# Four changes of emission order in a two-block transformer kernel on one core

## The chip, the cores and the metric

One core of one Trainium2 chip runs the whole kernel. Times are device microseconds (us) of one execution. Before the change the median of three runs is 884.3 us (883.33 to 884.74).

## The reference

A sequence of 256 rows of 1024 numbers (f32) goes through two blocks, one after the other. Cut to what the change touches, the first block computes:

```python
h = rmsnorm(x, g_mix_pre);  proj = h @ w_in
y_fox = forgetting_attention(fq, fk, fv, f_logit)         # 8 heads of 64
y_chk = chunked_relpos_attention(cq, ck, cv, rel_bias)    # 8 heads of 64
y = concat(rmsnorm(y_fox, g_fox_out), rmsnorm(y_chk, g_chk_out))
x = x + rmsnorm(y @ w_out, g_mix_post)
h = rmsnorm(x, g_mem_pre)
y = memory_cross_attention(h, rmsnorm(mem, g_mem_kv), w_mq, w_mk, w_mv, w_mo)  # 4 heads of 256
x = x + rmsnorm(y, g_mem_post);  h = rmsnorm(x, g_ff_pre)
y = square(relu(h @ w_ff1)) @ w_ff2
x = x + rmsnorm(y, g_ff_post)
```

The second block is a gated delta rule of 8 heads beside a sparse attention of 8 heads, an output product and a feed-forward part. Of it the change touches the values of the delta rule alone: they are transposed, scaled and stored (tile `vs`) before the first solve reads them.

## The kernel before

**Products.** All big products run on TensorE (PE). Each f32 weight tile (`raw`, 512 KB) comes by a DMA on SP's queue into one of four buffers and is split in two parts: ScalarE (ACT) writes `whi`, VectorE (DVE) then writes `wlo` = raw − whi. Each logical multiply is three matmuls (`mm3`): high by high, high by low, low by high. Activations are split the same way (`xhi`, `xlo`, or `xb`, which holds both). The 256 rows are two halves of 128, A and B. A product with rows as output (`gemm_n_skew`, tags `gs` and `mo`) computes all of half A first and then half B with the same weight parts, which are held in the meantime (`k.held`); `gemm_n_inter` (`gn`) alternates the halves. In both, `mm_n` does two steps of three 128x512 matmuls for one weight part, "a unit" below, with a `k.tick()` after each step.

**Order of the work.** The program is straight-line code, so each engine runs its instructions in the order in which Python emits them. Products are the main line. Everything else (heads, norms, transposes) is a generator, a "side": it runs until a `yield`, which names what it waits for. At each tick `Kern.tick` (L261) steps every side once whose due time has passed by a planner's clock, which advances with each emitted matmul by a fixed cost (three 128x512 matmuls are 0.64 us, three of 256 columns 0.32); the planner also keeps end times of ACT, DVE, POOL and DMA work. A yielded float means "due so many us after the clock now" (L253). Sides of rank −1 (the post chains) are stepped first. `k.finish` (L272) runs the named sides to their end at once, however late.

**Splits.** `Kern.pump` (L313) emits the `whi` and `wlo` of parts to come, each time the main line takes a part or drops a held one (`part`, `drop`). While a side of rank −1 lives it stops at four parts ahead. `refill` issues the DMA of the next raw tile when a split has been emitted. So the splits stand in the queues of ACT and DVE among the instructions of the chains, in the order of emission.

**What the change touches.**

- *Fox and chunked attention heads*, `head_pairs.rest` (L863 to 867): weights, transposes of `p` into a bank `tb`, DVE's copy to `pt`, then `attn_pv` (L671): three matmuls `o` from `pt` and the values. The heads run beside the `gt` products (steps of three 128x256 matmuls).
- *Post chains*, `chain_post` (L498 to 528) with `post_chain` (L976). For one half: squares of the product (`junk`, ACT), `yg` (DVE), a reciprocal root on POOL, `x` (DVE), squares again, `xg` (DVE), a second root `rs`, then `chain_xt` (L467): DVE scales `xg` by `rs` in place, PE transposes it in two groups of four (`tb`), and ACT and DVE split each group into `xb`. Two products use it ahead of a product that reads the result: `w_out` (`gs`, L990), after whose half B the second half of the memory values (`gn`, L991) fills PE before `k.finish(*st.values())` (L992) and the `mq` product (`gt`); and `w_mo` (`mo`), after which the feed-forward's `gs` follows, its half A behind `k.finish(st2[0])` (L1070) and its half B behind `k.finish(st2[1])` (`before_b`, L1073).
- *Memory heads and the `mo` product* (L998 and L1039 to 1059). Head 3 is the last; its `ops` matmuls are emitted as a side, and `k.finish(st[3])` stands before the units with i = 3, which read its output (`xhi`, `xlo` of `ot`). Half A: units (j, i) = (0,0), (0,1), (0,2), (1,0), (1,1), (1,2), then (0,3), (1,3); half B the same.
- *Values of the delta rule*, `chain_v` (L1622): for each of two groups and each half, four transposes of `vc` into `tb` and DVE's scaling into `vs`. `chain_gdn` (L1746) joins these sides before the first `solve`, whose matmuls are `wp`.

Of the kernel before, what the change touches and what calls it, by code (L numbers as in the profile page):

```python
# [23 lines left out]
A, B = 0, 1  # L24
# [14 lines left out]
def hs(half):  # L39
    return slice(half * P, half * P + P)  # L40
# [320 lines left out]
def split(k, hi, lo, src, scale=None):  # L361
    nc = k.nc
    if scale is None:
        nc.scalar.copy(hi, src)
        nc.vector.tensor_tensor(lo, src, hi.bitcast(F32), op=OP.subtract)
    else:
        nc.scalar.activation(hi, src, AF.Copy, scale=scale)
        nc.vector.scalar_tensor_tensor(lo, src, scale, hi.bitcast(F32), op0=OP.mult, op1=OP.subtract)
# [26 lines left out]
def mm_n(k, ps, xt, half, p, kt0, w=512, c0=0):  # L395

    for r in range(2):
        kt = kt0 + r
        for b, (a, e) in zip(ps, ((c0, c0 + w),) if len(ps) == 1 else ((0, w), (w, 2 * w))):
            k.mm3(b[:, :e - a], xt.x(kt, half), p.at(r, a, e), kt == 0, kt == KT - 1)  # L400
        k.tick()
# [48 lines left out]
def mean_sq(k, srcs, n):  # L450

    ss = k.small(2, "ss")
    for j, s in enumerate(srcs):
        k.nc.scalar.activation(k.junk[:, :s.shape[-1]], s, AF.Square, scale=n ** -0.5, accum_out=ss[:, j:j + 1])
    return ss


def transposes(k, srcs, n=P):

    ps = yield from k.get((P, 4, P), "tb")  # L460
    for j, s in enumerate(srcs):
        k.tr(ps[:, j, :n], s, n)
    yield ps
    return ps


def chain_xt(k, xt, half, xg, rs, kb0=0):  # L467

    nc = k.nc
    for j, g in enumerate(xg):  # L470
        if rs is not None:
            nc.vector.tensor_scalar(g, g, rs, None, op0=OP.mult)
    pend = []
    for j, g in enumerate(xg):
        yield g
        ps = yield from transposes(k, [g[:, i * P:i * P + P] for i in range(4)])
        split(k, xt.hi[kb0 + j][:, :, hs(half)], xt.lo[kb0 + j][:, :, hs(half)], ps)
        k.put()
    yield [t[kb0 + j][:, :, hs(half)] for t in (xt.hi, xt.lo) for j in range(len(xg))]
# [15 lines left out]
    yield from chain_xt(k, xt, half, xg, rs)  # L495


def chain_post(k, half, y, gpost, x_old, x_new, gpre, xt):  # L498


    nc = k.nc
    c = lambda t, j: t[:, j * 512:j * 512 + 512]
    yield y
    if gpost is not None:
        ss = mean_sq(k, y, D)
        yg = k.t4([P, D], name="yg")
        for j in range(2):
            nc.vector.tensor_tensor(c(yg, j), y[j], c(gpost, j), op=OP.mult)
        k.put(2)
        yield ss  # L510
        rs = rstd_col(k, ss, D)
        yield rs
    ss = k.small(2, "ss")
    for j in range(2):
        if gpost is not None:
            nc.vector.scalar_tensor_tensor(c(x_new, j), c(yg, j), rs, c(x_old, j), op0=OP.mult, op1=OP.add)
        else:
            nc.vector.tensor_tensor(c(x_new, j), y[j], c(x_old, j), op=OP.add)
        nc.scalar.activation(k.junk[:, :512], c(x_new, j), AF.Square, scale=D ** -0.5, accum_out=ss[:, j:j + 1])
    if gpost is None:  # L520
        k.put(2)
    xg = k.t4([P, D], name="xg")
    for j in range(2):
        nc.vector.tensor_tensor(c(xg, j), c(x_new, j), c(gpre, j), op=OP.mult)
    yield ss
    rs = rstd_col(k, ss, D)
    yield rs
    yield from chain_xt(k, xt, half, [c(xg, 0), c(xg, 1)], rs)


# [140 lines left out]
def attn_pv(k, pt, v0, v1, o0, o1):  # L671
    k.mm(o0, pt[:, 0], v0)
    k.mm(o1, pt[:, 1], v0, True, False)
    k.mm(o1, pt[:, 2], v1, False, True)
# [34 lines left out]
def block1(k, x, mem, w_in, b_fgt, rel, g_fox_out, g_chk_out, w_out, g_mix_pre, g_mix_post,  # L709
# [4 lines left out]
    x0 = [k.t4([P, D], name="x0") for _ in range(2)]  # L714
# [7 lines left out]
    ht = XT(k)  # L722
# [30 lines left out]
    ps = [norm_t(half, j) for half in range(2) for j in range(2)]  # L753
# [74 lines left out]
    fq, ev = qk_evac(0.125)  # L828
# [3 lines left out]
    fk, ev = qk_evac(1.0)  # L832
# [3 lines left out]
    y = [k.t4([P, D], name="y") for _ in range(2)]  # L836
# [25 lines left out]
    def head_pairs(scores, weights, v, o):  # L862
        def rest(h, s):  # L863
            p = yield from weights(h, s)
            pt = yield from attn_transpose(k, p, nc.vector.tensor_copy)
            c = slice(h * 64, h * 64 + 64)
            attn_pv(k, pt, v[:, 0, c], v[:, 1, c], o[0][:, c], o[1][:, c])

        def pair(i):
            s = yield from scores(i)  # L870
            yield from join([k.add(rest(2 * i + j, s[j])) for j in range(2)])
        return lanes(k, pair, 4, 3)
# [48 lines left out]
    cq, ev = qk_evac(0.125)  # L921
    gemm_t(k, ht, 512, ev)
    ck, ev = qk_evac(1.0)
# [47 lines left out]
    gpo, gmp = gain(k, g_mix_post), gain(k, g_mem_pre)  # L971
# [1 line left out]
    k.finish(s_fox)  # L973


    def post_chain(gpost, x_old, x_new, gpre_, xt):  # L976
        banks, st = {}, {}

        def evac(half, j, ps):
            banks[half, j] = ps[0]  # L980
            if j == 1:
                st[half] = k.add(chain_post(k, half, [banks[half, 0], banks[half, 1]], gpost, x_old[half],
                                            x_new[half], gpre_, xt), rank=-1)
            return True
        return evac, st

    x1 = x0
    ht = XT(k)
    ev, st = post_chain(gpo, x0, x1, gmp, ht)
    gemm_n_skew(k, yt, 2, ev, before_4=lambda: k.finish(s_chk))  # L990
    gemm_n_inter(k, mt, lambda half, ps: nc.scalar.copy(mv[half][:, 1], ps[0]))  # L991
    k.finish(*st.values())  # L992
# [3 lines left out]
    ot = XS(k)  # L996
# [33 lines left out]
    st = {}  # L1030
# [9 lines left out]
    x2 = x1  # L1040
    ht = XT(k)
    ev, st2 = post_chain(gmo, x1, x2, gfp, ht)
    parts = {}
    for half in range(2):
        ps = [k.bank(name="mo") for _ in range(2)]
        for js, iis in ((0, (0, 1, 2)), (1, (0, 1, 2)), (0, (3,)), (1, (3,))):
            if iis == (3,):
                k.finish(st[3])
            for i in iis:
                if half == 0:  # L1050
                    while (js, i) not in parts:
                        n = len(parts)
                        parts[n // 4, n % 4] = k.part()
                        k.held += 1
                else:
                    k.drop()
                mm_n(k, ps[js:js + 1], ot, half, parts[js, i], 2 * i)
        ev(half, 0, ps[0:1])
        ev(half, 1, ps[1:2])


    gfo2, gnx = gain(k, g_ff_post), gain(k, next_gain)
# [105 lines left out]
def block2(k, x3, ht, st, out, conv_w, norm_mlp_g):  # L1168
# [453 lines left out]
    def chain_v(b, sides):  # L1622
        yield from join(s_u)
        tp = yield from transposes(k, [kc[b][:, j, 0:P] for j in range(4)])
        nc.scalar.copy(kns[0][:, 4 * b:4 * b + 4], tp)
        k.put()
        yield from join(sides)
        for half in range(2):
            yield vc[b]
            tp = yield from transposes(k, [vc[b][:, j, hs(half)] for j in range(4)])  # L1630
            nc.vector.tensor_tensor(vs[half][:, 4 * b:4 * b + 4], tp, bc(hnk[:, half, 4 * b:4 * b + 4], P),
                                    op=OP.mult)
            k.put()
# [270 lines left out]
```

## Time and profile before

| | |
|---|---|
| median of the runs | 884.3 us |
| the profiled execution, its own time | 884.03 us |
| its span in the trace | 882.1 us |
| PE busy | 870.4 us (99%) |
| DVE busy | 603.5 us (68%) |
| ACT busy | 465.3 us (53%) |
| granted TensorE clock, whole span | 1.00 |

The span is the stretch from the first to the last instruction; 1.9 us of the execution's time lie outside it. The table says which engine has no room; where its few idle microseconds are, and who causes them, the waits and the timelines say. In a timeline a row is a run of like instructions, with the start of the first, and the number in brackets is the engine's idle time ahead of it and what ended that. The end of a matmul is modelled, so stretches are best read from start to start.

### The profile page before, as it was taken

The page shows a single profiled execution, that of the slowest core. Times are in us where ns is not written, and L with a number is a line of the kernel's source. Part 1 is how long each engine was busy: PE and PEld are TensorE (multiplying, and loading weights), DVE is VectorE, ACT ScalarE, POOL GpSimd, SP SyncE. Part 2 cuts the span into 40 slices and gives each one's busy share as a digit, 9 for nine tenths or more (in the row PEclk, how much of TensorE's full clock was granted, in tenths as well). Part 3 has the DMA queues.
Part 4 walks back from the last instruction along what each step waited for, and adds up shares of the span by engine and source line. Part 5 has one row for each costly group of instructions (what it writes and reads, how often), then busy time and mean ns, then how long its engine had stood idle before and what let it go on. Part 6 is the DMA issues. An engine that isn't in the chain of part 4 may idle for free.

```text
span 882.1 us, 13900 instructions
## 1 busy us (share of the span) xinstructions
PE 870.4 (99%) x5320; PEld 754.0 (85%) x5320; DVE 603.5 (68%) x1061; ACT 465.3 (53%) x837; POOL 89.2 (10%) x148
## 2 busy tenths in 40 slices
PE   7999999999999999999999999999999999999998
PEld 6979998799788888888798899988977888888887
DVE  5675664765687667664768999879567786666661
ACT  6574654554476444443648664553765564444440
POOL 3100010200020000000100138600010000000000
PEclk9999999999999999999999999999999999999999
DMA  8982436473387666654553586485235587666521
GB/s 268 294 246 77 144 120 239 119 262 99 94 242 218 207 201 191 191 191 146 172 161 97 143 188 182 97 230 155 71 95 173 165 252 200 191 191 191 192 96 48
DMA packets 162612, 150.82 MB, mean 171 GB/s; under 512 B 20081, under 2 KB 127217, under 8 KB 162546
## 3 DMA queue, kind: packets, MB, share of 16 engines
q1 hardware_dynamic: 161970, 148.88, 56.9%
q10 hardware_dynamic: 576, 1.05, 0.4%
q8 instruction: 42, 0.69, 0.3%
q14 instruction: 24, 0.20, 0.1%
HBM read 148.08 MB, written 1.84 MB: 170 GB/s over the span
## 4 chain that ended last, share of the span: by engine, by line
PE 90%; DVE 4%; ACT 4%; DMA 1%; issue 1%; POOL 0%; ACTq 0%; DVEq 0%; POOLq 0%
PE gt L212 33%; PE acc L212 20%; PE gn L212 12%; PE gs L212 11%; PE tb L225 3%; PE mo L212 3%; DVE wlo L96 2%; PE o L212 1%; ACT whi L96 1%; PE s L212 1%; PE ops L212 1%; PE ms L212 1%; ACT p L96 1%; DMA raw<-in_w_out_dram 1%; PE qp L212 1%
## 5 line engine op out<-in xcount | busy, mean ns | idle before, releaser
L96 DVE TENSOR_TENSOR wlo<-raw,whi 128x1024 fp32r<-128x1024 f32 (+1 forms) x263 | 315.9, 1224 | 107.9 <-ACT whi L96 98.8
L96 ACT CAST whi<-raw 128x1024 fp32r<-128x1024 f32 (+1 forms) x264 | 269.4, 1048 | 61.0 <-DMA raw<-in_w_in_dram 28.8
L212 PE MATMUL gt<-xb,whi 128*128 128x256 f32 (+1 forms) x1152 | 276.1, 322 | 0.0
L212 PE MATMUL gt<-xb,wlo 128*128 128x256 f32 x768 | 215.0, 280 | 0.0
L212 PEld LDWEIGHTS gt<-xb,whi 128*128 128x128 f32 x1152 | 189.9, 188 | 17.2 <-issue 0.3
L212 PEld LDWEIGHTS gt<-xb,wlo 128*128 128x128 f32 x768 | 144.7, 188 | 0.3
L212 PE MATMUL acc<-wlo,uh 128*128 128x512 f32 (+1 forms) x288 | 106.2, 369 | 0.0
L212 PE MATMUL acc<-whi,ul 128*128 128x512 f32 (+1 forms) x288 | 106.2, 369 | 0.0
L212 PE MATMUL acc<-whi,uh 128*128 128x512 f32 (+1 forms) x288 | 106.1, 368 | 0.0
L212 PE MATMUL gn<-whi,xb 128*128 128x512 f32 x256 | 90.2, 408 | 0.0
L212 PE MATMUL gs<-whi,xb 128*128 128x512 f32 (+1 forms) x288 | 86.3, 375 | 0.5 <-ACT xb L96 0.5
L212 PEld LDWEIGHTS acc<-whi,uh 128*128 128x128 f32 x288 | 54.2, 188 | 10.1
L212 PEld LDWEIGHTS acc<-whi,ul 128*128 128x128 f32 x288 | 54.1, 188 | 9.7
L212 PEld LDWEIGHTS acc<-wlo,uh 128*128 128x128 f32 x288 | 54.1, 188 | 9.5
L96 ACT COPY r<-gt 128x256 f32<-128x256 f32 x48 | 17.8, 370 | 84.0 <-PE gt L212 84.0
L212 PEld LDWEIGHTS gs<-whi,xb 128*128 128x128 f32 x288 | 51.9, 188 | 10.8 <-ACT xb L96 1.0
L212 PEld LDWEIGHTS gn<-whi,xb 128*128 128x128 f32 x256 | 48.2, 188 | 10.9 <-issue 1.0
L96 DVE TENSOR_TENSOR r<-gt,r 128x256 f32<-128x256 f32 x48 | 20.3, 423 | 49.7 <-ACT r L96 48.9
L212 PE MATMUL gs<-wlo,xb 128*128 128x512 f32 (+1 forms) x144 | 53.4, 371 | 0.8 <-DVE wlo L96 0.7
L96 POOL TENSOR_SCALAR ms<-ss 128x1 f32<-128x1 f32 x20 | 9.2, 459 | 422.1 <-ACT junk L96 422.0
L212 PE MATMUL gn<-wlo,xb 128*128 128x512 f32 x128 | 50.3, 393 | 0.0
L96 DVE SCALAR_TENSOR_TENSOR cy<-gt,cw,cy 128x255 f32<-128x255 f32 (+2 forms) x72 | 29.1, 474 | 4.7 <-ACT cy L96 4.6
(379 smaller groups left out, 1215.8 us busy)
## 6 DMA issues: line engine op xcount, KB each, us to landing
raw<-in_w_in_dram SPq DMA_DIRECT2D x84, 512.0 KB, 4.7
raw<-in_w_ff_dram SPq DMA_DIRECT2D x64, 512.0 KB, 4.7
raw<-in_w_mlp_up_dram SPq DMA_DIRECT2D x32, 512.0 KB, 5.6
raw<-in_w_mlp_down_dram SPq DMA_DIRECT2D x32, 512.0 KB, 3.4
raw<-in_w_out_dram SPq DMA_DIRECT2D x16, 512.0 KB, 3.8
raw<-in_w_mk_dram SPq DMA_DIRECT2D x8, 512.0 KB, 5.0
raw<-in_w_mv_dram SPq DMA_DIRECT2D x8, 512.0 KB, 4.0
raw<-in_w_mq_dram SPq DMA_DIRECT2D x8, 512.0 KB, 4.9
```

Of the source, the lines that this page charges most:

```text
L96: f(*args, **kw)
L212: self.nc.tensor.matmul(out, lhsT, rhs, start=start, stop=stop)
L225: self.nc.tensor.transpose(out, in_, self.ident[:n, :n])
```

## The change

Four edits. A side that is about to run `attn_pv` first waits 0.7 us of the planner's clock. The post chain of half A of the `w_out` product waits 2.0 us between its second root and `chain_xt`. In the `mo` product the first unit of half B moves ahead of half A's last two units and ahead of `k.finish(st[3])`. And each half of `chain_v` waits 2.5 us before its transposes.

```diff
@@ def chain_post @@
-def chain_post(k, half, y, gpost, x_old, x_new, gpre, xt):
+def chain_post(k, half, y, gpost, x_old, x_new, gpre, xt, later=0.0):
...
     rs = rstd_col(k, ss, D)
     yield rs
+    if later:
+        yield later
     yield from chain_xt(k, xt, half, [c(xg, 0), c(xg, 1)], rs)
@@ head_pairs.rest @@
             pt = yield from attn_transpose(k, p, nc.vector.tensor_copy)
             c = slice(h * 64, h * 64 + 64)
+            yield 0.7
             attn_pv(k, pt, v[:, 0, c], v[:, 1, c], o[0][:, c], o[1][:, c])
@@ post_chain @@
-    def post_chain(gpost, x_old, x_new, gpre_, xt):
+    def post_chain(gpost, x_old, x_new, gpre_, xt, later=0.0):
...
                 st[half] = k.add(chain_post(k, half, [banks[half, 0], banks[half, 1]], gpost, x_old[half],
-                                            x_new[half], gpre_, xt), rank=-1)
+                                            x_new[half], gpre_, xt, later * (half == A)), rank=-1)
...
-    ev, st = post_chain(gpo, x0, x1, gmp, ht)
+    ev, st = post_chain(gpo, x0, x1, gmp, ht, 2.0)
@@ the mo product @@
-    parts = {}
-    for half in range(2):
-        ps = [k.bank(name="mo") for _ in range(2)]
-        for js, iis in ((0, (0, 1, 2)), (1, (0, 1, 2)), (0, (3,)), (1, (3,))):
-            if iis == (3,):
-                k.finish(st[3])
-            for i in iis:
-                if half == 0:
-                    while (js, i) not in parts:
-                        n = len(parts)
-                        parts[n // 4, n % 4] = k.part()
-                        k.held += 1
-                else:
-                    k.drop()
-                mm_n(k, ps[js:js + 1], ot, half, parts[js, i], 2 * i)
-        ev(half, 0, ps[0:1])
-        ev(half, 1, ps[1:2])
+    parts, mo = {}, {}
+    first = [(js, i) for js in range(2) for i in range(3)]
+    last = [(0, 3), (1, 3)]
+
+    seq = [(A,) + x for x in first] + [(B,) + first[0]] + [(A,) + x for x in last]
+    seq += [(B,) + x for x in first[1:] + last]
+    for half, js, i in seq:
+        if (half, js, i) == (A, 0, 3):
+            k.finish(st[3])
+        if (half, js) not in mo:
+            mo[half, js] = k.bank(name="mo")
+        if half == A:
+            while (js, i) not in parts:
+                n = len(parts)
+                parts[n // 4, n % 4] = k.part()
+                k.held += 1
+        else:
+            k.drop()
+        mm_n(k, [mo[half, js]], ot, half, parts[js, i], 2 * i)
+        if (js, i) == (1, 3):
+            for j in range(2):
+                ev(half, j, [mo[half, j]])
@@ chain_v @@
         for half in range(2):
             yield vc[b]
+            yield 2.5
             tp = yield from transposes(k, [vc[b][:, j, hs(half)] for j in range(4)])
```

## Rows read from the trace of the kernel before

**Rows 1.** Page, part 1: busy time, share of the span, instructions per engine.

```profile
span 882.1 us, 13900 instructions
...
PE 870.4 (99%) x5320; PEld 754.0 (85%) x5320; DVE 603.5 (68%) x1061; ACT 465.3 (53%) x837; POOL 89.2 (10%) x148
```

**Rows 2.** Waits of PE: engine, line, awaited; total us, times, longest.

```profile
PE tb L225 <- DVE xg L96: 1.4, 2, 1.0
...
PE mo L212 <- ACT xhi L96: 0.7, 1, 0.7
```

**Rows 3.** Chain of waits: start us, length us, engine, operation (48 matmuls 128x512).

```profile
145.81 11.13 PE gs L212 x48
```

**Rows 4.** Timeline of PE, 64 to 70 us: start, duration, engine, operation, [idle before].

```profile
67.63 0.27 PE L212 MATMUL gt<-xb,wlo 128*128 128x256 f32 x1
68.40 1.55 PE L212 MATMUL o<-fv,pt 128*128 128x64 f32 x12 [0.49 <-DVE pt L96]
```

**Rows 5.** Timeline of DVE, 66 to 69.5 us.

```profile
67.79 1.48 DVE L96 COPY pt<-tb 128x384 f32<-128x384 f32 x3
```

**Rows 6.** Instructions on tile vs: duration min/median/max ns, first and last start us.

```profile
L212 PE MATMUL wp<-vs,TT x32: 270/275/276, 619.1 to 640.0; 128*128 128x128 f32 x32
...
L96 DVE TENSOR_TENSOR vs<-tb,hnk x4: 683/684/685, 571.0 to 591.1; 128x512 f32<-128x512 f32 x4
```

**Rows 7.** Timeline of PE, 163 to 168 us.

```profile
164.19 0.39 PE L212 MATMUL gs<-whi,xlo 128*128 128x512 f32 x1
165.57 0.63 PE L225 MATMUL tb<-ident,xg 128*128 128x128 f32 x4 [0.99 <-DVE xg L96]
```

**Rows 8.** Timeline of DVE, 156 to 186 us.

```profile
163.80 1.23 DVE L96 TENSOR_TENSOR wlo<-raw,whi 128x1024 fp32r<-128x1024 f32 x1 [0.68 <-ACT whi L96]
164.95 0.88 DVE L96 TENSOR_SCALAR xg<-xg,rs 128x512 f32<-128x512 f32 x2
...
177.56 0.88 DVE L96 TENSOR_SCALAR xg<-xg,rs 128x512 f32<-128x512 f32 x2
```

**Rows 9.** Timeline of PE, 177.5 to 182.5 us.

```profile
178.94 0.60 PE L225 MATMUL tb<-ident,xg 128*128 128x128 f32 x4
...
181.90 0.39 PE L212 MATMUL gt<-xb,whi 128*128 128x256 f32 x2
```

**Rows 10.** Timeline of PE, 224.5 to 231 us.

```profile
226.50 0.40 PE L212 MATMUL mo<-whi,xlo 128*128 128x512 f32 x1
226.92 1.99 PE L212 MATMUL ops<-mpt,mv 128*128 128x256 f32 x8
229.59 0.50 PE L212 MATMUL mo<-whi,xhi 128*128 128x512 f32 x1 [0.68 <-ACT xhi L96]
...
230.31 0.50 PE L212 MATMUL mo<-whi,xlo 128*128 128x512 f32 x1
```

**Rows 11.** Timeline of ACT, 226 to 258 us.

```profile
228.95 0.58 ACT L96 CAST xhi<-ops 128x512 fp32r<-128x512 f32 x1 [3.68 <-PE ops L212]
...
243.33 1.05 ACT L96 CAST whi<-raw 128x1024 fp32r<-128x1024 f32 x1
244.28 0.60 ACT L96 ACTIVATE junk<-mo 128x512 bf16<-128x512 f32 x1
...
253.45 1.05 ACT L96 CAST whi<-raw 128x1024 fp32r<-128x1024 f32 x1 [0.85 <-DMA raw<-in_w_ff_dram]
```

**Rows 12.** Timeline of PE, 244 to 258 us.

```profile
244.75 0.39 PE L212 MATMUL gs<-whi,xb 128*128 128x512 f32 x1
...
255.12 0.60 PE L225 MATMUL tb<-ident,xg 128*128 128x128 f32 x4
...
257.04 0.48 PE L212 MATMUL gs<-whi,xb 128*128 128x512 f32 x1
```

**Rows 13.** Timeline of DVE, 226 to 258 us.

```profile
229.57 0.69 DVE L96 TENSOR_TENSOR xlo<-ops,xhi 128x512 fp32r<-128x512 f32 x1 [2.70 <-ACT xhi L96]
...
253.56 0.94 DVE L96 TENSOR_SCALAR xg<-xg,rs 128x512 f32<-128x512 f32 x2
```

## The prediction

> **What bounds the kernel now.** I read the page's busy times first: PE works 870.4 of 882.1 us [rows 1], so all its idle time together is 11.7 us. No edit adds or removes a matmul or a DMA; all four can only move PE's idle time. The waits of PE say whose it is [rows 2]: transposes that waited for a scaled `xg` (two waits, 1.4 us, the longest 1.0) and the `mo` product that waited for `xhi` (0.7). The timelines place them. At 68.40 the value products `o` follow a step that started at 67.63 [rows 4]; at 165.57 transposes follow a matmul that started at 164.19 [rows 7]; around 227 to 230 the last memory head stalls the `mo` product [rows 10]. A 128x512 matmul takes 0.232 us from start to start (11.13 us for 48) [rows 3], which measures a gap better than the modelled ends.
>
> **What each stall is worth.** The first: the last 256-column matmul started at 67.63; with half of 0.232 its successor was due at 67.75, so 0.65 us are lost. The second: 164.19 + 0.23 = 164.42 against 165.57, 1.15 us. The third: from 226.50 + 0.23 = 226.73 to 230.31 + 0.23 = 230.54 there pass 3.81 us, and the work in them is eight `ops` (1.99 us by their row, some 1.7 until a next one could start, an estimate) and three `mo` matmuls (0.70), so about 1.4 to 1.5 us are lost. Together that is 3.3 us, the most that the change can win.
>
> **Edit 1, `o` later (−0.65).** 0.7 us of the planner's clock are three steps of 0.32, so `o` follows three more steps of three 256-column matmuls: 3 x 3 x 0.117 = 1.05 us. PE would come to `o` at 67.75 + 1.05 = 68.80. DVE copies three `pt` from 67.79 in 1.48 us, 0.49 each [rows 5], so the first two are there at 68.3 and 68.8. The stall goes. The wait is put into all 16 heads, but the others show no wait of this size, and the attention's ends have cover: the products that follow them start tens of steps later. Bounds: −0.65, and +0.3 if the later heads push one score or split by half a unit. I take −0.65, since the row shows `pt` ready in time.
>
> **Edit 4, values' transposes later (0).** DVE writes `vs` for the last time at 591.1, and its first reader on PE, `wp`, starts at 619.1 [rows 6]. A delay of 2.5 us per half, four in a chain at most 10 us, is hidden by the 28 us between; without that cover it would cost up to its 10. PE shows no wait at these transposes to win back. Bounds ±0.3, for reordering alone.
>
> **Edit 2, half A's scale and transposes 2.0 later (+0.6).** 2.0 us of the planner's clock are four ticks: 12 matmuls, 2.78 us. PE comes to the transposes at 164.42 + 2.78 = 167.20. But the yield stands ahead of DVE's scaling too, and while the main line goes on the pump puts two more `wlo` ahead of it. One `wlo` holds DVE 1.15 us (163.80 to 164.95), and the transposes started 0.62 us after the scaling did [rows 7, 8]. So the scaling starts at 164.95 + 2.30 = 167.25 and PE may go on at 167.87: a stall of 0.67 in place of 1.15, a gain of 0.5. Then the bill. The second group of transposes now falls behind the end of the product, and ACT and DVE split both groups about a microsecond later, just where half B's chain begins on the same queues. Its squares and `yg` shift by 1.1 us; by then one `wlo` more stands between `yg` and `x`. Its scaling goes from 177.56 [rows 8] by 1.1 + 1.15 to about 179.8, usable at 180.4. Before, PE reached half B's transposes at 178.94 [rows 9], some 0.9 us after they could start (177.56 + half of 0.88 = 178.0); in the new order they come behind the last memory-value matmul, with no product left between them and `mq`. Both groups are transposed back to back, and `mq`, which before started at 181.90 without a wait [rows 9], wants the split of the first. ACT's 0.6 and DVE's 0.7 for it are now in the open: an effective start of about 182.5. Net +0.6; bounds −1.15 (all as meant) and +1.2 (one more `wlo` ahead).
>
> **Edit 3, one unit of half B earlier (+2.1).** First its gain. PE runs three of the unit's six matmuls from 226.73 to 227.42, then `ops`, as its side is stepped at the tick inside the unit, then the other three to about 229.84. `ops` is 0.5 later than at 226.92, and so `xhi`, before from 228.95 to 229.53, and `xlo`, before from 229.57 to 230.26 [rows 11, 13]: the third matmul of unit (0,3) starts at 230.71 instead of 230.31 [rows 10], with 6 x 0.232 = 1.39 us of half B already done. The product ends 1.0 us earlier, at 243.75 instead of 244.75 [rows 12]. If `ops` stayed behind the whole unit this were 0.4, if no stall were left 1.4.
>
> Then what is late next. Half A's chain has one unit less of half B to hide behind. Its first transposes just make it into the last unit; the second group is forced behind the product by L1070, and their splits come on ACT and DVE in front of half B's squares. Those started at 244.28, right behind a `whi` of 243.33 [rows 11]; I put them at 245.4, 1.1 later, though their product ended 1.0 earlier. On DVE one more `wlo` (1.15) falls between `yg` and `x`, and ahead of the scaling two more `wlo` and the squaring of the feed-forward's first `r`; one of those `wlo` waits for a raw tile, as its `whi` did at 253.45 [rows 11]. I add 0.7 to 0.9. So the scaling goes from 253.56 [rows 13] by 1.1 + 1.15 + 0.8 to about 256.6, and the transposes, which PE could have begun at 254.1 (half of 0.94 on) and began at 255.12 [rows 12, 13], can begin at 257.0 to 257.3. PE by then is early: half A's `gs` ends at 243.75 + 11.13 = 254.88 [rows 3]. L1073 makes half B wait for them: 2.1 to 2.4 us of idle. The group and its split end so that half B's `gs` starts effectively at 258.6 to 258.9 against 256.61 (257.04 less 0.43 for the transposes of `r`, which move behind). Net +2.1, the lost 1.0 of the product's end included; bounds −1.4 (all as meant, half B's slack holds) and +2.4.
>
> **Sum.** −0.65 + 0 + 0.6 + 2.1 = +2.05. The profiled execution took 884.03, its span 882.1 and 1.9 around it; it is 0.3 under the median of 884.3. So 886.1 for that execution, 886.3 on the median. A measurement of this kernel can tell about 0.2%, 1.8 us, from no change: below 882.5 is faster, above 886.1 slower.
>
> **A rule beside it.** Edit 3's cover rests on 0.232 us per 128x512 matmul [rows 3]. The Trainium skill, "TensorE: Matmul & The Clock Gate", section "Back-to-back issue gap", gives about 131 ns for each of a sustained stream of 512 columns. By it the unit of six would hide 0.8 us instead of 1.39, an estimate from that page, and the sum would be some 0.6 higher. The trace does not agree with it, and the sum goes by the row.
>
> **Rivals.** (a) *As meant, faster.* Half B's transposes have 0.9 us of slack at 178.94 and 1.0 at 255.12 [rows 8, 9, 12, 13]. If the later half A delays half B's scaling by less than that, nothing is given back: −0.65 − 1.15 − 1.4, so 881.1, or 881.8 if edit 2's gain is the 0.5. It decides at one `wlo`: with none added ahead of half B's scaling it holds, with one of 1.15 it doesn't. For it: the splits are needed some time anyway, and an order that keeps them behind the chain costs PE nothing. Against: the pump emits at each unit, and DVE goes by that order. (b) *Half given back.* Edit 2 is paid for as above, but edit 3 keeps its 1.0, or the other way about with a small bill: −0.65 + 0.6 − 1.0 gives 883.3, at most 885.5. (c) *It doesn't do what it says.* The transposes' forced ends and the planner's slack undo edits 2 and 3 both, `ops` stays behind the whole unit: −0.65 + 0 − 0.4, so 883.3; near no change. (d) *Worse.* Half B's scaling falls a further `wlo` back in both places: 886.3 + 1.15 + 1.15 = 888.6.
>
> **How the numbers follow.** My forecast's case has 0.50, and its own range, from the bounds of the hidden terms, is 885.0 to 887.8; a fifth of it lies below 886.1. (a) has 0.22, (b) 0.14, (c) 0.08, (d) 0.06. Faster: 0.21 of (a) and 0.01 of (b), 0.22. Slower: 0.40 of the forecast and all of (d), 0.46. Same: the rest, 0.32. The range goes from 881.5, which leaves out about half of (a), to 887.8, which leaves out (d) and a little of the forecast.
>
> **What would show it.** Right: no wait at 68; the scaling of half A behind two more `wlo` and a wait of some 0.7 us at its transposes; half B's `w_out` transposes behind the last `gn`; `ops` between two groups of three half-B matmuls; the `mo` product ending 1.0 earlier; and a wait of PE for DVE's `xg` of about 2 us near 255, ahead of half B's `gs`. Wrong: if that last wait is below 0.5 us, edit 3 is a gain and the time falls below 884; if half B's scaling at about 178 stays within 0.9 us of its old place, edit 2 is a gain too, and (a) holds.

## The result and the profile after

The changed kernel takes 889.88 us (median of six runs, 889.56 to 890.42) against 884.08 (883.33 to 884.74) of the kernel before on the same chip: a ratio of 1.0067, interval 1.0054 to 1.0080. It is slower by 5.8 us where 2.05 were predicted, and lies 2.1 us above the top of the predicted range. The profiled execution took 889.56, its span 887.6.

Page, part 1, of the kernel after (the lines of [rows 1]):

```profile
span 887.6 us, 13905 instructions
...
PE 873.4 (98%) x5320; PEld 756.0 (85%) x5320; DVE 605.3 (68%) x1061; ACT 464.3 (52%) x837; POOL 85.5 (10%) x148
```

The work is the same: 5320 matmuls, 1061 instructions on DVE, 837 on ACT. PE's busy time grew by 3.0 us though no matmul was added, so some of them took longer or overlapped less; its idle time grew from 11.7 to 14.2. Both together are the span's 5.5.

Waits of PE in the kernel after, the whole span (total us, times, longest; the first row, for the gains' DMA at the start, is as before):

```profile
PE tb L225 <- ACT p L96: 2.2, 5, 1.3
PE tb L225 <- DVE xg L96: 1.4, 3, 0.5
...
PE gt L212 <- DVE xb L96: 0.3, 1, 0.3
PE gt L212 <- ACT xb L96: 0.3, 1, 0.3
```

Of the waits in [rows 2], the one for `xhi` is gone, and so is the one for `pt` in [rows 4]. The wait for weights `p` has grown (0.7 in total before, 2.2 now), and there are waits that weren't there: for both parts of `xb` ahead of a `gt`, and, in lines left out here, for a memory head's weights `mp` and their transposes `mpt`. To see where each microsecond arose, I paired the matmuls of the large products in order, the first `gt` with the first `gt` and so on, and took how much later each starts than in the kernel before. The lag counts from each trace's first matmul, and the table gives its median in some stretches of the kernel before (in us from its span's start). A jitter of up to 1.2 us in the first 60 us of an execution is in each row's first columns, so what matters is the steps along a row.

| kernel | 30–50 | 150–158 | 184–190 | 216–220 | 245–250 | 262–280 | 605–618 | 655–664 | 860–875 |
|---|---|---|---|---|---|---|---|---|---|
| after (all four edits) | 0.09 | −0.84 | −0.03 | 1.19 | 0.34 | 2.92 | 2.92 | 6.29 | 5.62 |
| edit 1 alone | 0.34 | 0.82 | 0.84 | 0.89 | 0.87 | 0.89 | 1.05 | 0.99 | 0.96 |
| edit 2 alone | 0.23 | 0.19 | 0.87 | 2.06 | 2.08 | 2.04 | 2.12 | 2.12 | 2.54 |
| edit 3 alone | 0.13 | 0.09 | 0.13 | 0.13 | −0.73 | 1.74 | 1.76 | 1.75 | 1.62 |
| edit 4 alone | 1.09 | 1.48 | 1.52 | 1.52 | 1.54 | 1.54 | 1.52 | 4.59 | 4.01 |

The first row falls by 0.9 behind the fox heads (edit 1). It rises by 0.8 to the `mq` product and by 1.2 more over the memory heads (edit 2). It falls by 0.9 over the `mo` product and rises by 2.6 inside the feed-forward's `gs` (edit 3). Near 650 it rises once more, by 2.7 that stay (edit 4). The rows of the trace show each of these places.

**Edit 1.** Timeline of PE at 67 to 70 us, kernel after (answers to [rows 4]):

```profile
68.80 1.45 PE L212 MATMUL o<-fv,pt 128*128 128x64 f32 x12
```

No bracket at `o`: the wait has gone, and `o` starts at the predicted 68.80. DVE's copies `pt` start at 67.78 (67.79 in [rows 5]).

**Edit 2.** Timeline of DVE at 160 to 182 us, kernel after (answers to [rows 8]):

```profile
162.87 3.50 DVE L96 TENSOR_TENSOR wlo<-raw,whi 128x1024 fp32r<-128x1024 f32 x3 [0.68 <-ACT whi L96]
166.29 0.87 DVE L96 TENSOR_SCALAR xg<-xg,rs 128x512 f32<-128x512 f32 x2
...
178.78 0.88 DVE L96 TENSOR_SCALAR xg<-xg,rs 128x512 f32<-128x512 f32 x2
```

Timeline of PE at 160 to 184 and at 213 to 219 us, kernel after (its first rows answer to [rows 7, 9]):

```profile
166.91 0.63 PE L225 MATMUL tb<-ident,xg 128*128 128x128 f32 x4 [0.50 <-DVE xg L96]
...
179.60 1.03 PE L225 MATMUL tb<-ident,xg 128*128 128x128 f32 x8
...
181.65 0.39 PE L212 MATMUL gt<-xb,whi 128*128 128x256 f32 x1 [0.34 <-DVE xb L96]
...
214.61 0.41 PE L225 MATMUL tb<-ident,mp 128*128 128x128 f32 x2 [0.36 <-DVE mp L96]
215.54 2.00 PE L212 MATMUL ops<-mpt,mv 128*128 128x256 f32 x8 [0.52 <-DVE mpt L96]
217.18 0.58 PE L212 MATMUL mo<-whi,xhi 128*128 128x512 f32 x1
```

Three `wlo` stand in a row ahead of half A's scaling where one stood; both groups of half B's transposes (x8) lie ahead of `mq` with no product behind them, and the splits of `xb` are in the open. Up to here this is the predicted picture, a microsecond early by edit 1. The last three rows are not in the prediction. Before the `mo` product PE now waits 0.36 for `mp` and 0.52 for `mpt` of a memory head, with nothing between its transposes at 214.61 and its `ops`; in the kernel before, there were nine matmuls of `gt` between a head's transposes and its `ops` and no wait there, and `mo` began at 216.07.

**Edit 3.** Timeline of PE at 226 to 260 us, kernel after (answers to [rows 10, 12]):

```profile
227.91 0.39 PE L212 MATMUL mo<-whi,xhi 128*128 128x512 f32 x1
...
228.60 1.89 PE L212 MATMUL ops<-mpt,mv 128*128 128x256 f32 x8
230.13 0.58 PE L212 MATMUL mo<-whi,xhi 128*128 128x512 f32 x1
...
255.87 0.50 PE L212 MATMUL gs<-wlo,xb 128*128 128x512 f32 x1 [0.74 <-DVE wlo L96]
...
257.12 0.60 PE L225 MATMUL tb<-ident,r 128*128 128x128 f32 x4
258.22 1.11 PE L225 MATMUL tb<-ident,xg 128*128 128x128 f32 x8 [0.49 <-DVE xg L96]
```

Timeline of DVE in the same stretch, kernel after (answers to [rows 13]):

```profile
257.66 0.90 DVE L96 TENSOR_SCALAR xg<-xg,rs 128x512 f32<-128x512 f32 x2
```

`ops` lies between two groups of three matmuls of half B, as predicted, and half B's scaling comes at 257.66 against 253.56 in [rows 13]. The one wait of about 2 us for `xg` came as two: 0.74 for a `wlo` inside half A's `gs`, and 0.49 for `xg`, with the transposes of `r` at 257.12 between them. Half B's `gs` then starts at 259.55, against 257.04 in [rows 12].

**Edit 4.** Instructions on tile `vs`, kernel after (the first and the last row answer to [rows 6]; `op` are the delta rule's output products, one name per group and half):

```profile
L212 PE MATMUL wp<-vs,TT x32: 272/276/276, 622.7 to 643.9; 128*128 128x128 f32 x32
...
L212 PE MATMUL op__6715<-vs,QE x8: 275/276/276, 635.8 to 636.6; 128*128 128x128 f32 x8
...
L212 PE MATMUL op__6720<-vs,QE x8: 275/276/276, 636.7 to 637.5; 128*128 128x128 f32 x8
...
L96 DVE TENSOR_TENSOR vs<-tb,hnk x4: 680/683/685, 575.6 to 592.5; 128x512 f32<-128x512 f32 x4
```

The values are in time: the last is written at 592.5, the first reader starts at 622.7. Yet `op` of the two groups now follow each other (635.8 and 636.7), where in the kernel before they ran 2.8 us apart (633.2 and 636.0). What that does is seen in the timeline of ACT at 640 to 662 us, here of the kernel before. `junk<-qs` are squares for the norm of a delta-rule output, four to a group, `p` are the exponentials of a head of the sparse attention:

```profile
644.01 0.31 ACT L96 ACTIVATE junk<-qs__6733 128x128 bf16<-128x128 f32 x1 [1.33 <-DVE qs__6733 L96]
...
646.96 0.49 ACT L96 ACTIVATE p<-lg,nmx,asc 128x128 f32<-128x128 f32 x1 [1.25 <-DVE nmx L96]
...
652.63 0.31 ACT L96 ACTIVATE junk<-qs__6764 128x128 bf16<-128x128 f32 x1
```

The same view of the kernel after:

```profile
649.85 0.31 ACT L96 ACTIVATE junk<-qs__6778 128x128 bf16<-128x128 f32 x1 [4.52 <-DVE qs__6778 L96]
...
652.89 0.31 ACT L96 ACTIVATE junk<-qs__6780 128x128 bf16<-128x128 f32 x1
...
653.20 0.48 ACT L96 ACTIVATE p<-lg,nmx,asc 128x128 f32<-128x128 f32 x1
```

Before, one group's squares came ahead of the heads' `p` and the other's behind them, and the first `p` started as soon as DVE's `nmx`, the last thing that it needs, was there. After, all eight squares run from 649.85 to 653.20 and the `p` stand behind them. Their input was there long before. Timeline of DVE in the same stretch, kernel after:

```profile
650.94 0.16 DVE L96 TENSOR_TENSOR nmx<-mx,nasc 128x2 f32<-128x2 f32 x1
```

So the first `p` stood 2.1 us in ACT's queue with its input ready (651.10 to 653.20), behind squares. Timeline of PE at 650 to 660 us, kernel after:

```profile
652.13 0.39 PE L212 MATMUL gn<-whi,xb 128*128 128x512 f32 x1
653.83 0.33 PE L225 MATMUL tb<-ident,p 128*128 128x128 f32 x1 [1.30 <-ACT p L96]
...
655.87 0.78 PE L212 MATMUL gn<-whi,xb 128*128 128x512 f32 x1
656.44 0.63 PE L212 MATMUL gn<-wlo,xb 128*128 128x512 f32 x1
656.87 0.63 PE L212 MATMUL gn<-whi,xb 128*128 128x512 f32 x1
```

Windows of the same stretch, kernel after (length, then busy us of PE, PEld, DVE, ACT and POOL with their instructions, the granted clock, DMA share, GB/s):

```profile
652.00:654.00 2.00, 0.70 (x4) 0.23 (x2) 0.00 (x0) 1.91 (x9) 0.00 (x0) 1.00 0.09 36
...
656.00:658.00 2.00, 2.00 (x9) 1.60 (x8) 0.00 (x0) 2.00 (x6) 1.97 (x2) 0.50 0.00 0
658.00:660.00 2.00, 2.00 (x8) 1.60 (x8) 1.93 (x5) 1.16 (x4) 0.00 (x0) 0.71 0.00 0
```

PE waits four times for `p`, 2.0 us in all, while ACT is busy 1.91 of 2 us, mostly with squares. All waits of PE from 590 to 690 us come to 2.4 us, and to 1.0 in the kernel before: 1.4 more. Then the granted clock goes to 0.50, which is the level of 1.2 GHz, and matmuls start 0.43 us apart (656.44 to 656.87) instead of 0.232 [rows 3]. Until 659.20, when the starts are 0.23 apart again, six such matmuls and three transposes took 3.3 us from 655.87 on; at the spacings of the same trace outside this stretch (0.23 for such a matmul, 0.32 for the first behind transposes, 0.11 for a transpose) they would have taken 1.8, an estimate: 1.5 more. The 1.4 and the 1.5 together come near the 2.7 us of this trace; they are not quite independent, since a slower PE finds a later `p` ready.

### The profile page after: what moved, and what is told of

Same layout as the page of the kernel before. It is cut to its first block, busy times and chain, and to the rows that moved or that the text cites. A ratio compares the mean times of both kernels' runs of the same rounds, so it can differ in the third digit from the quotient of the medians.

```text
span 887.6 us, 13905 instructions
## 1 busy us (share of the span) xinstructions
PE 873.4 (98%) x5320; PEld 756.0 (85%) x5320; DVE 605.3 (68%) x1061; ACT 464.3 (52%) x837; POOL 85.5 (10%) x148
## 3 DMA queue, kind: packets, MB, share of 16 engines
q10 hardware_dynamic: 576, 1.05, 0.4%
## 4 chain that ended last, share of the span: by engine, by line
PE 90%; DVE 4%; ACT 3%; issue 1%; DMA 0%; POOL 0%; ACTq 0%; DVEq 0%; POOLq 0%
PE gt L212 32%; PE acc L212 20%; PE gn L212 12%; PE gs L212 11%; PE tb L225 3%; PE mo L212 3%; DVE wlo L96 2%; ACT junk L96 1%; PE s L212 1%; PE o L212 1%; ACT whi L96 1%; PE ops L212 1%; PE ms L212 1%; PE ao L212 1%; PE yp L212 0%
## 5 line engine op out<-in xcount | busy, mean ns | idle before, releaser
L212 PEld LDWEIGHTS gs<-wlo,xb 128*128 128x128 f32 x144 | 27.2, 189 | 6.7 <-DVE wlo L96 2.5
```

The source lines that it names most:

```text
L212: self.nc.tensor.matmul(out, lhsT, rhs, start=start, stop=stop)
```

## The experiments

### The four edits, each alone

Each kernel is the one before with a single edit of the diff above:

```diff
@@ only_o_later: head_pairs.rest, ahead of attn_pv @@
+            yield 0.7
@@ only_scale_later: chain_post, behind yield rs, for half A of w_out @@
+    if later:
+        yield later
@@ only_unit_early: the mo product @@
+    seq = [(A,) + x for x in first] + [(B,) + first[0]] + [(A,) + x for x in last]
+    seq += [(B,) + x for x in first[1:] + last]
@@ only_vt_later: chain_v, ahead of the transposes @@
+            yield 2.5
```

> The kernel before with the 0.7 us ahead of the value products alone. Theory (four edits add up, each in its own stretch): the stall of 0.65 us at 68 us goes and nothing moves behind it, so 0.7 to 0.9 us below before, about 883.3. Rival (the loss of 2.8 us that the changed kernel shows between 590 and 660 us comes from an order that an early edit passes on): above 885.

> The kernel before with the 2.0 us in the first post chain alone. Theory: half A's scaling falls behind two more splits, half B's chain and the memory heads behind it are late, so 1.5 to 2.2 us above before, about 886, all of it gathered by 216 us. Rival (the edit is a gain, and the lateness at 180 to 216 us is the first edit's): 0.5 to 1.1 us below before, about 883.3.

> The kernel before with the new order of the mo product alone. Theory: the product ends 0.9 to 1.4 us earlier, half B's post chain is late behind it and PE waits near 255 us, so 1.3 to 2.1 us above before, about 886, all of it gathered by 262 us. Rival (that wait comes from the lateness of the second edit, not from this one): 1.0 to 1.4 us below before, about 883.

> The kernel before with the 2.5 us ahead of the values' transposes alone. Theory: the two groups of the delta rule, which ran one step apart, run in the same steps, their squares stand together on ACT ahead of the last heads' exponentials, PE waits for those and its clock falls: 2.5 to 3.0 us above before, about 886.8, all of it between 590 and 666 us, with the granted clock at 0.5 in part of it. Rival (my prediction's step: these transposes have cover, and the loss there was passed on from the first block): within 0.3 us of before.

Measured, beside 884.07 of the kernel before on the same chip:

| edit alone | median us | ratio (interval) | difference | predicted |
|---|---|---|---|---|
| 1, `o` later | 883.79 | 1.0000 (0.9991 to 1.0009) | −0.28 | −0.65 |
| 2, scale later | 886.38 | 1.0027 (1.0016 to 1.0037) | +2.31 | +0.6 |
| 3, unit early | 885.64 | 1.0020 (1.0011 to 1.0029) | +1.57 | +2.1 |
| 4, values later | 886.83 | 1.0036 (1.0022 to 1.0050) | +2.76 | 0 |

The four differences sum to 6.4, the change as a whole makes 5.8: they nearly add up, so each can be studied by itself. Edit 1's median can't be told from nothing, and falls short of the 0.7 to 0.9 that was expected of it. Its profiled execution had a wait of 1.3 us for DVE's `ncum` near 60 us, which the kernel before lacks in its own and which hides the gain in the table of lags; step by step the lag of this trace is 1.73 ahead of 68 us and 1.00 behind 82, so 0.7 is won there.

Edit 2 alone shows both of its places again without edit 1's shift. DVE at 163 to 181 us, edit 2 alone:

```profile
167.28 0.88 DVE L96 TENSOR_SCALAR xg<-xg,rs 128x512 f32<-128x512 f32 x2
...
179.78 0.88 DVE L96 TENSOR_SCALAR xg<-xg,rs 128x512 f32<-128x512 f32 x2
```

The prediction had 167.25 and 179.8. In its row of the lags the step to `mq` is 0.68, and that over the memory heads another 1.2. Edit 4 is by its median the largest loss, with no need of the others; in its trace the clock fell as well (0.64 in 652 to 654 us, 0.51 in 654 to 656).

### Edit 4: is it the values' lateness, or the order of the two groups?

Two theories: the values' chain is late and something waits for it; or the wait of 2.5 shifts the planner so that both groups' later steps fall together, and their squares block ACT. The first kernel keeps edit 4 and holds the second group back; the second kernel drops edit 4 and brings the groups together by another wait.

```diff
@@ vt_later_apart: edit 4, and in gdn(b), behind its first yield @@
+        if b:
+            yield 2.0
@@ groups_together: without edit 4; in gdn(b), behind yield vd @@
+        if b == 0:
+            yield 0.7
```

> The values' transposes 2.5 us later, as in the changed kernel, and the second group of the delta rule 2.0 us of the planner's clock behind the first, so that the squares of its last step stand behind the last heads' exponentials on ACT again. Theory (the loss of 2.8 us is the two groups' squares, eight in a row, ahead of those exponentials): it goes, within 0.7 us of before, about 884.3. Rival (the loss is the later transposes themselves, whose values come later to the solves): still 2 to 3 us above before.

> The kernel before, no edit of the change in it, with the first group of the delta rule held back 0.7 us of the planner's clock so that both groups run in the same steps and their last squares stand together ahead of the last heads' exponentials. Theory (order on ACT): 1.5 to 3 us above before, with PE idle for ACT's p near 650 us and a lower granted clock behind it. Rival (the transposes' lateness): within 0.5 us of before.

With the groups apart: 885.72 beside 884.32, ratio 1.0018 (1.0009 to 1.0027), +1.4 us, where at most 0.7 was expected. About half of the loss came back (this interval and that of edit 4 alone just overlap), the clock stayed at 1.00, and the waits of PE in 590 to 690 us were short:

```profile
PE tb L225 <- ACT p L96: 1.3, 5, 0.3
PE ao L212 <- ACT pt L96: 0.4, 1, 0.4
```

Where the other half arises was not traced.

With the groups together and no edit 4: 884.81, ratio 1.0007 (0.9998 to 1.0015), +0.5 us, less than was expected for it. Its eight squares do stand in a row, from 646.04 to 649.08, but ahead of the place where the `p` are due: the longest wait for `p` is 0.7. The first `p` starts there at 650.47, when DVE's `nmx` is ready, and not behind a square (DVE itself had waited 1.57 for these squares just before, so this kernel is not free of them). So eight squares in a row are not enough to cost 2.8 us; what this kernel lacks is a `p` that is ready and stands behind them. Lateness of `vs` can't be the cause in either kernel: PE waits for `vs` at most 0.2 us.

### Edit 4: which of its waits tips the order

The same 2.5 in only one of the two halves. If the delay as such cost time, either half should show part of it.

```diff
@@ vt_a_later: chain_v, ahead of the transposes @@
+            if half == 0:
+                yield 2.5
@@ vt_b_later: the same place @@
+            if half == 1:
+                yield 2.5
```

> The kernel before with the 2.5 us ahead of the values' transposes of half A alone. No transposes come later than in the changed kernel, and half B's last come no later than before by more than a step, but the planner emits both groups of the delta rule in the same steps again. Theory (order): 2 to 3 us above before, about 886.5, with the exponentials behind eight squares and a granted clock near 0.5 behind PE's wait. Rival (lateness): at most half of the full edit's 2.8 us, below 885.5.

> The kernel before with the 2.5 us ahead of the values' transposes of half B alone. The order of everything from 595 us on stays that of before. Theory (the order of emission costs, not the transposes' lateness, which has the cover that I gave it): within 0.5 us of before, clock 1.00. Rival (values that come later make the solves late): 1 us or more above before.

Half A's wait: 886.78 beside 883.46, ratio 1.0040 (1.0026 to 1.0053), +3.3: the whole loss. Half B's wait: 883.39, ratio 0.9999 (0.9990 to 1.0008): nothing. With half B's wait `op` of the two groups stay 2.8 us apart (633.5 and 636.3), as in the kernel before; with half A's they follow each other (633.0 and 633.9). A limit of this pair: with half B's wait DVE's last write of `vs` came at 588.4, before the 591.1 of [rows 6], so it delays the values less than half A's does (592.2); it is the order that splits the two kernels, but not the order alone that differs.

Timeline of PE in half A's kernel, at 648 to 654 us:

```profile
651.00 0.33 PE L225 MATMUL tb<-ident,p 128*128 128x128 f32 x1 [1.26 <-ACT p L96]
```

Windows of the same stretch of that kernel (columns as above):

```profile
650.00:652.00 2.00, 0.75 (x3) 0.34 (x3) 0.00 (x0) 1.94 (x9) 0.00 (x0) 1.00 0.00 0
652.00:654.00 2.00, 1.56 (x8) 0.94 (x7) 0.95 (x7) 1.63 (x7) 0.85 (x1) 1.00 0.00 0
```

The waits are those of the kernel after, and I expected the clock to fall too. In this trace it did not, and the kernel is as slow. So the fall of the clock is not needed for the loss; the waits of PE from 590 to 690 us come to 3.0 us in this trace, 2.0 more than before, for a lag that grew by 2.5. In the lags of this kernel the step near 650 is 2.4 (0.90 to 3.25) against 3.1 and 3.4 in the two traces with the fall (edit 4 alone, after); by 860 us they stand at 2.5, 2.5 and 2.7 above their values at 605.

### Edit 4: can the squares go elsewhere?

If the squares in front of the `p` are the cause, moving them behind the `p` should give the loss back; the rival was that what waits for the squares comes late in its turn.

```diff
@@ squares_behind: edit 4, and in gdn_o, behind its second yield o (half B) @@
+            yield 1.4
```

> The values' transposes 2.5 us later, as in the changed kernel, with both groups still in the same steps, and the squares of the groups' last step 1.4 us of the planner's clock later, so that all eight stand behind the three heads' exponentials on ACT. Theory (PE waits for those exponentials, which stand behind the eight squares though their inputs are there 2 us earlier, and its clock falls in the wait): the clock stays at 1.00 and at least 2 of the 2.8 us come back, 884.0 to 884.9. Rival (the groups' lateness on DVE and PE, not the squares): 1 us or less comes back, 885.8 or more.

894.58 beside 883.73, ratio 1.0124 (1.0109 to 1.0140): +10.9, far worse than either theory had it. The wait for `p` did go. Waits of PE in 590 to 690 us of that kernel:

```profile
PE tb L225 <- DVE Z L96: 5.5, 2, 4.0
PE ao L212 <- ACT pt L96: 1.6, 2, 1.4
PE tb L225 <- ACT p L96: 0.5, 2, 0.3
```

At 655 to 664 us its lag is 2.83, against 4.59 with edit 4 alone (at 605 to 618 they stood at 1.2 and 1.5). So some 1.6 us of loss remain there of 3.1; the steps in this stretch stand in another order, which makes the median a rough one. But ACT's copies `pt` come late, the last head's `p` starts at 666.95 (663.44 with edit 4 alone), and DVE's merge of the outputs (`oat`, `Z`), which the output product needs, starts at 674.43 instead of 667.76, when PE has nothing left. The clock did not stay at 1.00 either: behind that wait it was granted at 0.50 from 678 to 684 us. So at its place the theory holds for about half of the loss, and this kernel does not show what the change would cost without the squares in front: 1.4 later they are in the way of something else.

### Edit 2: the wait, or the splits ahead of the scaling?

The same wait of 2.0, but behind DVE's scaling instead of ahead of it, so that the `wlo` emitted in the meantime come after `xg`; and the same with edit 1.

```diff
@@ scaled_first: chain_xt, behind the scaling of xg by rs; later is 2.0 for half A of w_out @@
+    if later:
+        yield later
@@ o_later_scaled_first: this, and edit 1 in head_pairs.rest @@
+            yield 0.7
```

> The kernel before with the 2.0 us of the second edit behind DVE's scaling instead of ahead of it, so that only the transposes move. Theory (the second edit costs because two splits slip ahead of the scaling in DVE's queue): the wait of 1.0 us at 165 us goes and no split stands ahead of half B's scaling that did not before, so 0.6 to 1.2 us below before, about 883.1. Rival (the second group of half A's transposes behind the product delays half B's chain on ACT anyway): 0.5 us above before or more.

> The first edit, and the second one's wait behind the scaling. Theory: both stalls go, 0.65 and 1.15 us, about 1.5 us below before, 882.6. Rival (as for the two alone): at or above before.

scaled_first: 884.75 beside 884.32, ratio 1.0004 (0.9995 to 1.0013), where edit 2 had +2.31. The loss is gone; the gain of 0.6 to 1.2 that was expected did not come. Timeline of DVE at 160 to 182 us of this kernel:

```profile
165.80 0.87 DVE L96 TENSOR_SCALAR xg<-xg,rs 128x512 f32<-128x512 f32 x2
166.59 2.35 DVE L96 TENSOR_TENSOR wlo<-raw,whi 128x1024 fp32r<-128x1024 f32 x2
...
178.59 0.88 DVE L96 TENSOR_SCALAR xg<-xg,rs 128x512 f32<-128x512 f32 x2
```

Timeline of PE of the same kernel, 163 to 170 us:

```profile
166.65 0.60 PE L225 MATMUL tb<-ident,xg 128*128 128x128 f32 x4
```

The scaling comes at 165.80, behind one `wlo`; two more `wlo` follow it, and PE finds `xg` ready at 166.65. (With edit 2's own place it came behind all three, at 167.28.) Half B's scaling comes at 178.59 in place of 179.78. The lag falls from 0.86 at 150 us to 0.14 at `mq`: 0.7 are won there; the memory heads take back 0.4 by 216 us and the rest of the kernel most of what is left (0.74 at 860 us). With edit 1 it is 883.71, ratio 0.9989 (0.9980 to 0.9998): faster than the kernel before by 0.6 us, of 1.5 expected, where the change is slower by 5.8. It is the only version here whose interval lies below 1, and it does so barely.

### Edit 3: hold the splits back

In the prediction the `wlo` in front of half B's chain are edit 3's price. This kernel is edit 3 with the pump stopped at one part ahead, instead of four, from the end of the `mo` product until half B's transposes are through (`gap` is 4, and 1 in that stretch).

```diff
@@ splits_held: edit 3, and Kern.pump @@
-            if self.n_split - self.n_used >= 4 and any(s.rank < 0 for s in self.sides):
+            if self.n_split - self.n_used >= self.gap and any(s.rank < 0 for s in self.sides):
```

> The new order of the mo product, as in the changed kernel, and the pump held at one part ahead instead of four from the end of that product until half B's post chain is done. Theory (half B's scaling is late by the splits that stand ahead of it on DVE): it comes 2 to 3 us earlier, near 254 us, PE's wait for it goes, and if the parts last the time is 0.5 to 1.0 below before, 883.5. Rival (PE has no room for later splits either): waits of PE for wlo in half A's or B's gs take its place, and the time stays 1 us or more above before.

886.57 beside 883.73, ratio 1.0036 (1.0024 to 1.0049), +2.8: no better than edit 3 alone (+1.6; the two intervals overlap). Timeline of PE at 249 to 256 us of this kernel:

```profile
250.37 0.50 PE L213 MATMUL gs<-whi,xb 128*128 128x512 f32 x1 [0.70 <-ACT whi L96]
251.62 0.50 PE L213 MATMUL gs<-wlo,xb 128*128 128x512 f32 x1 [0.76 <-DVE wlo L96]
```

Timeline of DVE of the same kernel:

```profile
252.72 0.94 DVE L96 TENSOR_SCALAR xg<-xg,rs 128x512 f32<-128x512 f32 x2
```

The scaling comes four microseconds earlier than with edit 3 alone (256.67) and the wait for `xg` is gone. But half A's `gs` now waits for the splits themselves, three times (the third, of 0.34, at 255.45), 1.8 us. The rival named for this run was right: in this stretch DVE, busy 15.05 of the 17 us from 245 to 262 in the kernel before, has little room for both: with the scaling first, PE waited for the splits instead.

## Why the prediction was wrong

The sign was right, the size was not: of the 3.75 us between +5.8 and +2.05, the runs put +2.8 on edit 4, +1.7 on edit 2, −0.5 on edit 3 and +0.4 on edit 1, and −0.6 on the way they combine.

**Edit 4, the step that failed.** "A delay of 2.5 us per half, four in a chain at most 10 us, is hidden by the 28 us between", with "±0.3, for reordering alone". The first half held: the values were done at 592.5, their reader came at 622.7, and no wait for them passes 0.2 us. But in a program whose engines run in order of emission, a wait in one side also decides in which step all later instructions of that side are emitted, and beside what. Cover in time says nothing on that. The two groups, whose `op` had been 2.8 us apart, followed each other at 0.9; more than fifty microseconds behind the edit, eight squares stood on ACT ahead of the exponentials that PE waited for, the first of which had its input 2.1 us before it started. Half A's wait alone gives the whole loss, half B's none, and holding the groups apart gives about half of it back. What the order costs depends on the place: groups_together has the same eight squares in a row for +0.5. The term for "reordering alone" was therefore a guess without a row behind it. A bound from rows was to be had: PE waits for `p` already in the kernel before, so `p` has no slack there, and one group's four squares take 1.7 us of ACT (644.01 to 645.71 in its trace).

**Edit 2, right up to `mq`, then a term was missing.** Scaling at 167.28 (167.25), a wait of 0.66 from start to start (0.67; the row's 0.49 counts from a modelled end), half B's scaling at 179.78 (179.8), `mq`'s second start at 182.63 (182.5): each step as worked out, and +0.68 measured for +0.6. The sum stopped there. Behind `mq` the memory heads were taken to run as before, only later; but their `ms`, transposes and `ops` fall into other steps of the product, and ahead of `mo` PE waits 0.36 and 0.52 for a head with nothing in between. That is +1.2, the same oversight as in edit 4 on a smaller scale. That it was the `wlo` ahead of the scaling, as the prediction had it, and not the wait as such, is shown by scaled_first: the same wait behind the scaling costs nothing that can be measured.

**Edit 3, right in mechanism, 0.5 too large.** The product ended 0.9 earlier (`gs` at 243.84 alone, 243.75 predicted); the scaling came at 256.67 (256.6); half B's `gs` started at 258.56 (258.6). The wait was split: 0.76 of it fell on a `wlo` inside half A's `gs`, which the prediction saw as DVE's delay but not as PE's, and 0.50 on `xg`. The 0.5 that is too much lies in one term: the sum took 0.43 off the old start of 257.04 because the transposes of `r` would move behind, but they ran at 256.13, inside the wait, so the new start is 1.5 later than the old and not 2.0. +1.57 measured for +2.1. The sign that was to tell a gain, a wait for `xg` below 0.5 near 255, misleads: in the kernel after that wait is 0.49 and the edit is a loss all the same, since the rest of the idle time stood elsewhere. Rival (a), that slack would swallow the later chain, and (b) and (c) are out: half B's scaling came 3.1 later than before, behind the `wlo` as was said. Rival (d), a further `wlo` in both places, gave 888.6, near the measured time, but its mechanism was not found.

**Edit 1, right at its place.** `o` at 68.80 without a wait, 0.9 won by 150 us in the trace of the kernel after, 0.7 in its own. Alone it is too small to be seen in the median (−0.28, interval of about ±0.8).

**The rule beside the sum.** The unit of six in edit 3 ran at the row's 0.23 from start to start in the kernel after too (227.91 to 228.60 for three). The Trainium skill, "TensorE: Matmul & The Clock Gate", section "Back-to-back issue gap", has 131 ns for such a matmul in a stream; by that the end of the product would have come 0.4 earlier, an estimate from that page, and the trace, with 0.9, does not agree.

**What stays open.** Which due time in the planner puts the two groups into the same step was not traced, nor why holding them apart leaves 1.4 us. How edit 4's loss divides between the waits and the slower clock differs from trace to trace; no kernel was run that keeps one without the other by design.

## What to carry to other kernels

In straight-line code with interleaved sides, cost a wait twice: by the slack of what it delays, and by what else is emitted in other steps because of it, on every engine and far behind the edit; the second is read by comparing the order of instructions ahead of the tightest waits, not from cover. Where a wait is inserted into a chain, put it behind the short instruction that frees the next engine: filler that is emitted during the wait (here splits of 1.15 us) goes ahead of everything the chain still has to issue. And where two engines are nearly full in a stretch, holding one kind of work back can just rename the wait, as in splits_held.

## What the hardware showed that was not expected

Between 652.36 and 655.87 PE ran only six transposes, with waits for ACT (1.30, 0.26, 0.18, 0.26) between them; then the granted clock was 0.50 from 656 to 658 us and 0.71 from 658 to 660, and matmuls of 512 columns started 0.43 us apart instead of 0.232. The Trainium skill, "TensorE: Matmul & The Clock Gate", section "Wait — 56ns, not 53.3ns?", gives 426.7 ns for 512 columns at 1.2 GHz; the trace agrees. With nearly the same waits (1.26, 0.25, 0.18, 0.26) in the kernel with half A's wait alone, the clock stayed at 1.00. So these traces do not show whether such a stretch brings the clock down. The kernel with edit 4 whole, with the fall in its trace, took 886.83 (+2.8 on its chip), and the one with half A's wait, without it, 886.78 (+3.3 on its own).
